# Attention scores: the rests of the keys kept twice, each copy on one half of the partitions with zeros on the other, so that both products of a head read 128 rows

## The chip, the cores and the metric

The kernel runs on one core of one Trainium2 chip. The metric is the device time of one execution in microseconds (us), the median over runs. Five engines work side by side: TensorE (PE; its weight loads are shown apart as PEld), VectorE (DVE), ScalarE (ACT), GpSimd (POOL) and SyncE (SP), which issues most of the DMAs.

## The reference, cut to what matters

Two transformer blocks are computed for 256 tokens of width 1024. The change lies in the attention of the first block. It has eight heads of 64 columns and two groups of keys and values, four heads to a group. For every query there are three sets of scores, each followed by a softmax and a weighted sum of values:

```python
logits_c = einsum('bgrsd,bgnd->bgrsn', qg, kc) * scale + bias    # 15 compressed keys
logits_s = einsum('bgrqd,bgqkd->bgrqk', q_b, ks) * scale + bias_s  # selected blocks
logits_w = einsum('bgrqd,bkgd->bgrqk', q_b, kw) * scale + bias     # window
o = g[..., 0:1] * o_c + g[..., 1:2] * o_s + g[..., 2:3] * o_w
```

Each score is a sum over the 64 columns of one head. All data are float32.

## The kernel before, in words

TensorE multiplies float32 numbers here in a shorter form (F32R). To keep the accuracy, every operand is split in a rounded part and a rest (`split`, lines 362 to 364: ACT copies the rounded part, DVE or POOL subtracts it from the source). A full product is then made of three: rounded by rounded, rounded by rest, rest by rounded (`mm3`).

**How the scores are laid out.** For head `h` the tile `q[:, h]` has the rounded queries on one half of its 128 partitions (the lower half for even heads, the upper one for odd heads) and the rests of the same queries on the other half (lines 858 to 860). The tile `k` of a branch (`ks` for the selected blocks, `kw` for the window) has two planes: plane 0 the rounded keys, the same on both halves, plane 1 the rests of the keys, the same on both halves (lines 866 to 872). The compressed keys `kc` are laid out in the same way (lines 765 and 766). So `dots` (lines 957 to 961) makes two products for each head: all 128 rows of `q` with plane 0, which gives the rounded queries and their rests times the rounded keys, and then 64 rows of `q`, the half with the rounded queries, with 64 rows of plane 1. The second takes 64 rows because the other half of `q[:, h]` holds rests, which must not be multiplied with the rests of the keys.

**Order around it.** `attend(tt)` is a generator for 128 queries. It is called for the second half of the tokens first (256 keys, `ns` is 2) and then for the first half (128 keys). Each makes one group of scores for `kc` (8 heads, 16 columns each) and then the groups of `ks` and `kw`: two groups of four heads each per branch for 256 keys, one group of eight heads per branch for 128 keys. A group begins with products of `flip` and `wp`, which put the bias into PSUM (line 1013), and goes on with `dots`. In a pair of heads (one even, one odd) the order is: 128 rows, 64 rows, 128 rows, 64 rows. The score groups write to PSUM tiles tagged `y` (4 buffers, 2 to a group), and `soft` (DVE maxima, ACT exponentials) of a group is issued behind the `dots` of the next group.

Between two groups `run(t)` puts filler work onto TensorE: the projections of the convolution branch (`conv_part`, products `pb<-hT,hl`) and later the output projection. How much is decided while the program is built, from planned prices (`AC`, `AS`, `AX_`, `AP`, `AP0`) and the planner's own count of the filler's time (`self.pe`); the products of `dots` are not in that count. In this stage only ACT's order is written by hand; the order of the other engines is the scheduler's. The filler's weights come over `Stream`: a DMA into 4 raw buffers, then a split into 3 buffers `hl`.

**Tiles touched.** `pct` (line 1041) is the tile that the compressed softmax is spread into, twice per call of the kernel, in a pool of its own (`sm`, 2 buffers). The pool `work` has a tag `xs` with 2 buffers of 128 x 1024, used by the norm at the start of the block and by the one at its end (`start`, `boundary`, `lead`).

Of the kernel before, what the change touches and what calls it, by code (L numbers as in the profile page):

```python
# [10 lines left out]
F32 = mybir.dt.float32  # L11
F32R = mybir.dt.float32r
# [3 lines left out]
AF = mybir.ActivationFunctionType  # L16
# [325 lines left out]
class Kern:  # L342
# [381 lines left out]
    def compress(self, p, pe, which):  # L724

        nc = self.nc
        z = self.tmp.tile([128, 2, 256], F32, tag="z", name=self.name("z"), bufs=2)
        for g in range(2):
            nc.scalar.activation(z[0:64, g], p[g * 64:(g + 1) * 64, :256], AF.Copy)
            nc.vector.tensor_copy(z[64:128, g, 0:255], p[g * 64:(g + 1) * 64, 1:256])  # L730
        blk = self.tmp.tile([128, 16, 2, 15], F32, tag="blk", name=self.name("blk"), bufs=2)
        for hf in range(2):
            src = z[:, :, 16 * hf:16 * hf + 240].rearrange("p g (n l two) -> p l g n two", l=8, two=2)[:, :, :, :, 0]
            b = self.vs(pe, 8 * hf, 8)
            for g in range(2):
                nc.vector.tensor_add(blk[:, 8 * hf:8 * hf + 8, g], src[:, :, g], b[:, :, None].to_broadcast([128, 8, 15]))  # L736
        br = self.tmp.tile([128, 2, 16, 30], F32R, tag="br", name=self.name("br"), bufs=2)
        bv = blk.rearrange("p l g n -> p l (g n)")
        self.split(br[:, 0], br[:, 1], bv)
        yield  # L740
        hid = self.tmp.tile([128, 2, 2, 16], F32, tag="hid", name=self.name("hid"), bufs=2)
        nc.gpsimd.memset(hid, 0.0)
        ph = self.pb()
        for i in range(4):
            w = self.st.get().rearrange("p h (l c) -> p h l c", l=4)
            for j in range(4):
                self.mm3(ph[:30, :256], (br[:, 0, 4 * i + j], br[:, 1, 4 * i + j]), (w[:, 0, j], w[:, 1, j]),
                         i + j == 0, i + j == 6)
            if i == 1:
                yield  # L750
        hr = self.tmp.tile([30, 256], F32, tag="hr", name=self.name("hr"), bufs=2)
        nc.scalar.activation(hr, ph[:30, :256], AF.Gelu_apprx_tanh)
        yield
        p = self.pb()
        for ht in range(2):
            self.tr(p[:, ht * 32:ht * 32 + 30], hr[:, ht * 128:(ht + 1) * 128])
        for ht in range(2):
            nc.vector.tensor_copy(hid[:, ht, :, :15], p[:, ht * 32:ht * 32 + 30].rearrange("p (g n) -> p g n", g=2))
        yield
        p2 = self.pb()  # L760
        if which == "k":
            for ht in range(2):
                self.mm(p2[:, :32], self.w2[:, ht, :128],
                        hid[:, ht].rearrange("p g n -> p (g n)"), ht == 0, ht == 1)
            self.kc = self.attn.tile([128, 2, 32], F32R, name="kc")
            self.split(self.kc[:, 0], self.kc[:, 1], p2[:, :32])
        else:
            hv = self.tmp.tile([128, 2, 2, 4, 16], F32, name="hv")
            for ht in range(2):
                nc.vector.tensor_copy(hv[:, ht], hid[:, ht][:, :, None, :].to_broadcast([128, 2, 4, 16]))  # L770
            for ht in range(2):
                self.mm(p2[:, :64], hv[:, ht].rearrange("p g r n -> p (g r n)"), self.w2[:, ht, 128:], ht == 0, ht == 1)
            self.vcb = self.attn.tile([128, 2, 64], F32, name="vcb")
            nc.vector.tensor_mul(self.vcb, p2[:, :64][:, None, :].to_broadcast([128, 2, 64]),
                                 self.c("hpar")[:, :, None].to_broadcast([128, 2, 64]))
# [42 lines left out]
    def block1(self, ctx):  # L818
        tc, nc, A = self.tc, self.nc, self.A
# [21 lines left out]
        with tc.manual_schedule(engines={mybir.EngineType.PE}):  # L841
# [11 lines left out]
            q = self.attn.tile([128, 8, 256], F32R, tag="q", name="q", bufs=1)  # L853
            for i in range(4):
                p = self.proj(self.st.get(), hT, S)
                for j in range(2):
                    r, o = slice(64 * j, 64 * j + 64), slice(64 - 64 * j, 128 - 64 * j)
# [5 lines left out]
        kd, vt = {}, {}  # L863
        for br in "sw":
            p = self.proj(self.st.get(), hT, S)
            k = self.attn.tile([128, 2, 2, 256], F32R, name=f"k{br}")
            for g in range(2):
                r = slice(g * 64, g * 64 + 64)
                o = slice(64 - g * 64, 128 - g * 64)
                self.split(k[r, 0, g], k[r, 1, g], p[r, :256])  # L870
                nc.scalar.activation(k[o, 0, g], k[r, 0, g].bitcast(F32), AF.Copy)
                nc.vector.tensor_copy(k[o, 1, g], k[r, 1, g].bitcast(F32))
            kd[br] = k.rearrange("p a g s -> p a (g s)")
            next(cv, None)
        pv = [self.pb(), self.pb()]
        for k0, k1 in VVG:
            w = self.st.get().rearrange("p h (k c) -> p h k c", c=280)
            for tt in range(2):
                t = slice(tt * 128, tt * 128 + 128)
# [15 lines left out]
        sm = ctx.enter_context(tc.tile_pool(name="sm", bufs=1))  # L895
# [52 lines left out]
        def half(h):  # L948
            return slice((h % 2) * 64, (h % 2) * 64 + 64)

        def attend(tt):
# [3 lines left out]
            t = slice(tt * 128, tt * 128 + 128)  # L955

            def dots(out, heads, k, c0, n, stop):
                for o, h in zip(out, heads):
                    r = half(h)
                    self.mm(o, q[:, h, t], k[:, 0, c0:c0 + n], False, False)  # L960
                    self.mm(o, q[r, h, t], k[r, 1, c0:c0 + n], False, stop)

            P = sm.tile([128, 2, 8, sw], F32, tag=f"P{tt}", name=self.name("P"), bufs=1)
            nm = self.small.tile([128, 16], F32, tag="nm", name=self.name("nm"), bufs=2)
# [3 lines left out]
            p = self.py()  # L968
            for j in range(2):
                o = p[:, 512 * j:512 * j + 64].rearrange("p (h n) -> p h n", h=4)  # L970
# [3 lines left out]
            for i in range(4):  # L974
                dots([p[:, 512 * j + 16 * i:512 * j + 16 * i + 16] for j in range(2)], (2 * i, 2 * i + 1), self.kc,
                     i // 2 * 16, 16, i == 3)
# [28 lines left out]
            for b, br in enumerate("sw"):  # L1005
                for gi in range(0, len(groups), 2):
                    y = self.py()
                    pv = [y[:, 512 * j:512 * j + 512].rearrange("p (h s) -> p h s", h=nh) for j in range(2)]
                    hss = groups[gi:gi + 2]
                    for j in range(2):  # L1010
                        hs = hss[j]
                        for hl in range(2):
                            self.mm(pv[j], self.flip, self.wp[:, hl, hs[0]:hs[-1] + 1:2, 256 - sw:256], hl == 0, False)
                    for i in range(nh):
                        hs = [hss[j][i] for j in range(2)]
                        dots([o[:, i] for o in pv], hs, kd[br], hs[0] // 4 * 256, sw, i == nh - 1)
                    late()
                    late = lambda b=b, hss=hss, pv=pv: soft(b, hss, pv)
                    yield AS
# [18 lines left out]
            p = self.pb()  # L1038
            self.tr(p[:, :128], pc.rearrange("p h n -> p (h n)"))
            late()  # L1040
            pct = sm.tile([128, 4, 128], F32, tag="pct", name=self.name("pct"), bufs=2)
            nc.vector.tensor_mul(pct, p[:, None, :128].to_broadcast([128, 4, 128]),
                                 self.c("hpair")[:, :, None].to_broadcast([128, 4, 128]))
            scale(*steps[0])
# [48 lines left out]
        with tc.manual_schedule(engines={E.Activation}):  # L1093
            a1, a0 = attend(1), attend(0)
            for t in till_none(a1):
                run(t)
            first = till_none(a0)
            for t in a1:
                run(t)
                t = next(first, None)  # L1100
                if t is not None:
                    run(t)
            for t in first:
                run(t)
            scored = True
            w3 = self.attn.tile([128, 3, 2, 1024], F32R, tag="wp", name="w3", bufs=1)
            w1 = self.attn.tile([128, 2, 1024], F32R, tag="q", name="w1", bufs=1)
            w2 = sm.tile([128, 2, 2, 1024], F32R, tag="P1", name="w2", bufs=1)
            self.st.spare = [w3[:, 0], w3[:, 1], w3[:, 2], w1, w2[:, 0], w2[:, 1]]
            for t in a0:  # L1110
                run(t)
            for _ in fl:
                pass
# [931 lines left out]
```

## Time and profile before

| what | value |
|---|---|
| median of 3 runs | 1535.54 us (1530.86 to 1537.42) |
| the profiled execution, its own time | 1540.11 us |
| its span in the profile | 1538.4 us |
| granted TensorE clock, mean over the span | 0.972 |
| PE busy | 1455.4 us (95%) |
| DVE, ACT, POOL busy | 1067.6, 807.3, 280.9 us |
| the stage of the scores | about 71 to 153 us |

The rows further down are from one profiled execution. In the timeline, each row is a run of like instructions: its start, the time from the first one's start to the last one's end, engine, line, operation, tiles written and read, the shape of the first of them, and their count. Matmuls overlap, so the time that one takes from TensorE is read as the start of the next row less the start of this one, by the count. Line 371 is the helper `mm`, through which nearly all products go.

### The profile page before, as it was taken

The page shows a single profiled execution, that of the slowest core. Times are in us where ns is not written, and L with a number is a line of the kernel's source. Part 1 is how long each engine was busy: PE and PEld are TensorE (multiplying, and loading weights), DVE is VectorE, ACT ScalarE, POOL GpSimd, SP SyncE. Part 2 cuts the span into 40 slices and gives each one's busy share as a digit, 9 for nine tenths or more (in the row PEclk, how much of TensorE's full clock was granted, in tenths as well). Part 3 has the DMA queues.
Part 4 walks back from the last instruction along what each step waited for, and adds up shares of the span by engine and source line. Part 5 has one row for each costly group of instructions (what it writes and reads, how often), then busy time and mean ns, then how long its engine had stood idle before and what let it go on. Part 6 is the DMA issues. An engine that isn't in the chain of part 4 may idle for free.

```text
span 1538.4 us, 29510 instructions
## 1 busy us (share of the span) xinstructions
PE 1455.4 (95%) x11884; PEld 1325.3 (86%) x11884; DVE 1067.6 (69%) x1979; ACT 807.3 (52%) x1282; POOL 280.9 (18%) x138
## 2 busy tenths in 40 slices
PE   5999899999888869998999999999999999999997
PEld 4979799998777768978999899999999998888886
DVE  6765777777579992974990699884555556777766
ACT  4734565555463344644445577774444445444554
POOL 3100320004353423025698200000000000000000
PEclk9998999999899989999999999999999999999999
DMA  6622445555332212354477444547555557877773
GB/s 206 238 91 76 149 164 181 192 183 201 117 114 67 79 56 76 131 193 141 159 227 231 156 166 159 169 158 219 192 183 188 191 191 270 244 243 242 241 243 127
DMA packets 93024, 263.50 MB, mean 171 GB/s; under 512 B 10271, under 2 KB 34975, under 8 KB 92760
## 3 DMA queue, kind: packets, MB, share of 16 engines
q1 hardware_dynamic: 77200, 243.80, 48.6%
q10 hardware_dynamic: 15688, 17.83, 3.4%
q8 instruction: 93, 1.52, 0.4%
q14 instruction: 43, 0.35, 0.1%
HBM read 247.67 MB, written 13.91 MB: 170 GB/s over the span
## 4 chain that ended last, share of the span: by engine, by line
PE 75%; DVE 16%; ACT 4%; DMA 2%; issue 2%; POOL 1%; SPq 0%; ACTq 0%; DVEq 0%; POOLq 0%
PE pb L371 39%; PE py L371 35%; DVE acc L1247 4%; DVE hl L364 2%; ACT hl L363 1%; PE pb L383 1%; DMA raw<-in_ws_dram 1%; POOL hl L364 1%; DVE m L1869 1%; DVE nc L425 0%; DMA x<-in_x_dram 0%; DVE blk L736 0%; ACT junk L515 0%; DVE nc L426 0%; DMA cst<-in_cst_dram 0%
## 5 line engine op out<-in xcount | busy, mean ns | idle before, releaser
L371 PE MATMUL pb<-hT,hl 128*128 128x256 f32 (+1 forms) x4944 | 630.8, 286 | 10.6 <-DVE qT L364 5.2
L371 PEld LDWEIGHTS pb<-hT,hl 128*128 128x128 f32 x4944 | 612.0, 192 | 19.2 <-issue 6.3
L363 ACT ACTIVATE hl<-raw 128x1024 fp32r<-128x1024 f32 x412 | 434.2, 1054 | 232.5 <-issue 162.8
L364 DVE TENSOR_TENSOR hl<-raw,hl 128x1024 fp32r<-128x1024 f32 (+1 forms) x317 | 389.3, 1228 | 111.1 <-ACT hl L363 110.9
L371 PE MATMUL py<-hl,coef 128*128 128x512 f32 x1536 | 356.4, 390 | 0.2 <-DVE coef L364 0.2
L371 PEld LDWEIGHTS py<-hl,coef 128*128 128x128 f32 x1536 | 285.5, 188 | 59.7 <-DVE coef L364 0.6
L364 POOL TENSOR_TENSOR hl<-raw,hl 128x1024 fp32r<-128x1024 f32 x95 | 236.8, 2499 | 354.7 <-ACT hl L363 234.1
L1922 ACT ACTIVATE act<-pb 128x256 f32<-128x256 f32 x128 | 49.3, 385 | 166.1 <-PE pb L371 166.1
L2001 POOL TENSOR_TENSOR end<-end,end 128x512 f32<-128x512 f32 x2 | 2.6, 1279 | 665.0 <-DVE end L1999 663.5
L371 PE MATMUL py<-hT,hl 128*128 128x272 f32 (+1 forms) x768 | 118.2, 304 | 1.6 <-POOL hl L364 1.6
L371 PEld LDWEIGHTS py<-hT,hl 128*128 128x128 f32 x768 | 103.5, 198 | 8.3 <-issue 4.8
L364 DVE TENSOR_TENSOR coef<-act,coef 128x256 fp32r<-128x256 f32 x128 | 54.0, 423 | 72.5 <-ACT coef L363 72.5
L1926 DVE TENSOR_TENSOR act<-act,G 128x256 f32<-128x256 f32 x128 | 53.8, 420 | 34.4 <-ACT act L1922 33.2
L1247 DVE SCALAR_TENSOR_TENSOR acc<-UU,vt,acc 128x256 f32<-128x256 f32 x120 | 75.5, 670 | 0.7
L1882 ACT ACTIVATE G<-py 128x512 f32<-128x512 f32 x64 | 67.4, 1143 | 3.0 <-PE py L371 3.0
L1869 DVE TENSOR_TENSOR m<-e,gg 128x1536 bf16<-128x1536 bf16 x64 | 60.6, 953 | 0.7
L371 PE MATMUL py<-m,e 128*128 128x128 bf16 x768 | 52.8, 219 | 1.0 <-DVE m L1869 0.9
L363 ACT ACTIVATE coef<-act 128x256 fp32r<-128x256 f32 x128 | 51.7, 404 | 3.3 <-DVE act L1926 3.3
L1865 DVE TENSOR_TENSOR e<-gi,iota 128x1024 bf16<-128x1024 bf16 x64 | 43.6, 688 | 12.6 <-PE py L371 12.5
L371 PEld LDWEIGHTS <-e 128*128 128x128 bf16 x768 | 44.3, 97 | 4.4 <-DVE m L1869 2.4
L371 PE MATMUL py<-hl,gu 128*128 128x512 f32 x192 | 47.3, 393 | 0.4 <-DVE hl L364 0.2
L371 PEld LDWEIGHTS py<-hl,gu 128*128 128x128 f32 x192 | 34.9, 188 | 7.7 <-DVE hl L364 0.5
(416 smaller groups left out, 1380.7 us busy)
## 6 DMA issues: line engine op xcount, KB each, us to landing
raw<-in_ws_dram SPq DMA_DIRECT2D x172, 512.0 KB, 3.4
raw<-in_ut_dram SPq DMA_DIRECT2D x128, 512.0 KB, 3.4
raw<-in_ev_dram SPq DMA_DIRECT2D x128, 512.0 KB, 4.2
ad<-act ACTq DMA_DIRECT2D x90, 128.0 KB, 3.1
act<-ad SPq DMA_DIRECT2D x90, 128.0 KB, 3.1
wf<-fd ACTq DMA_DIRECT2D x2, 800.0 KB, 4.9
x<-in_x_dram SPq DMA_DIRECT2D x2, 512.0 KB, 6.1
xd<-x ACTq DMA_DIRECT2D x1, 1024.0 KB, 4.2
```

The lines of the kernel that those rows point to most:

```text
L363: self.nc.scalar.activation(h, src, AF.Copy)
L364: (eng or self.nc.vector).tensor_sub(l, src, h.bitcast(F32))
L371: self.nc.tensor.matmul(out, lhsT, rhs, start=start, stop=stop, skip_group_check=True)
L383: self.nc.tensor.transpose(out, in_, self.ident[p0:p0 + n, p0:p0 + n])
L1247: nc.vector.scalar_tensor_tensor(acc[:, i], UU[:, i, 16 + j:272 + j], self.v("cw", 4 * j + i), acc[:, i], op0=OP.mult, op1=OP.add)
L1865: nc.vector.tensor_tensor(e.rearrange("p c a i j -> p (c a) i j"), gi[:, b].rearrange("p c (a j) -> p (c a) j", j=2)[:, :, None, :].to_bro ...
L1869: nc.vector.tensor_mul(m, e[:, 0][:, None].to_broadcast([128, 3, 2, 128, 2]), gg[:, b].rearrange("p k (a j) -> p k a j", j=2)[:, :, :, Non ...
L1882: nc.scalar.activation(G[:, :, 4 * b:4 * b + 4].rearrange("p a t -> p t a"), p.rearrange("p (t a) -> p t a", t=4), AF.Copy)
L1922: nc.scalar.activation(a, p[:, :S], AF.Gelu)
L1926: nc.vector.tensor_mul(a, a, self.G[:, c])
L2001: nc.gpsimd.tensor_mul(t[:, tt], x[:, tt, cols[1]], g[:, cols[1]])
```

## The change

`k` gets three planes: plane 0 as before, plane 1 with the rests on the lower half and zeros on the upper one, plane 2 with zeros on the lower half and the rests on the upper one. POOL writes the zeros; ACT and DVE write the same number of copies as before. `kc` gets three planes in the same way; its rest is now made by two DVE subtractions of 64 partitions each in place of one of 128. The second product of `dots` takes all 128 rows of `q` with plane 1 for even heads and plane 2 for odd heads, so the half of `q` with rests meets zeros. `pct` moves from its own tag to the tag `xs` of the pool `work`.

```diff
-            self.kc = self.attn.tile([128, 2, 32], F32R, name="kc")
-            self.split(self.kc[:, 0], self.kc[:, 1], p2[:, :32])
+            self.kc = self.attn.tile([128, 3, 32], F32R, name="kc")
+            nc.gpsimd.memset(self.kc[:, 1:].bitcast(F32), 0.0)
+            nc.scalar.activation(self.kc[:, 0], p2[:, :32], AF.Copy)
+            for j in range(2):
+                r = slice(64 * j, 64 * j + 64)
+                nc.vector.tensor_sub(self.kc[r, 1 + j], p2[r, :32], self.kc[r, 0].bitcast(F32))
...
-            k = self.attn.tile([128, 2, 2, 256], F32R, name=f"k{br}")
+            k = self.attn.tile([128, 3, 2, 256], F32R, name=f"k{br}")
             for g in range(2):
                 r = slice(g * 64, g * 64 + 64)
                 o = slice(64 - g * 64, 128 - g * 64)
-                self.split(k[r, 0, g], k[r, 1, g], p[r, :256])
+                nc.gpsimd.memset(k[o, 1 + g].bitcast(F32), 0.0)
+                self.split(k[r, 0, g], k[r, 1 + g, g], p[r, :256])
                 nc.scalar.activation(k[o, 0, g], k[r, 0, g].bitcast(F32), AF.Copy)
-                nc.vector.tensor_copy(k[o, 1, g], k[r, 1, g].bitcast(F32))
+                nc.vector.tensor_copy(k[o, 2 - g, g], k[r, 1 + g, g].bitcast(F32))
...
                 for o, h in zip(out, heads):
-                    r = half(h)
                     self.mm(o, q[:, h, t], k[:, 0, c0:c0 + n], False, False)
-                    self.mm(o, q[r, h, t], k[r, 1, c0:c0 + n], False, stop)
+                    self.mm(o, q[:, h, t], k[:, 1 + h % 2, c0:c0 + n], False, stop)
...
-            pct = sm.tile([128, 4, 128], F32, tag="pct", name=self.name("pct"), bufs=2)
+            pct = self.work.tile([128, 8, 128], F32, tag="xs", name=self.name("pct"), bufs=2)[:, :4]
```

## Rows read from the trace of the kernel before

**Rows 1.** The page: the chain that ended last, shares of the span by engine.

```profile
PE 75%; DVE 16%; ACT 4%; DMA 2%; issue 2%; POOL 1%; SPq 0%; ACTq 0%; DVEq 0%; POOLq 0%
```

**Rows 2.** Busy time by stretch; columns: stretch, length, each engine's busy time, clock, DMA.

```profile
50.00:71.30 21.30, 20.49 (x165) 18.99 (x164) 18.45 (x29) 14.54 (x24) 4.21 (x2) 1.00 0.65 217
71.30:99.40 28.10, 28.10 (x161) 22.67 (x160) 14.74 (x34) 14.25 (x38) 0.00 (x0) 1.00 0.34 124
99.40:131.50 32.10, 32.10 (x162) 27.76 (x161) 17.75 (x50) 10.58 (x35) 0.00 (x0) 0.79 0.20 66
...
153.00:170.00 17.00, 14.82 (x75) 11.28 (x74) 14.34 (x23) 13.20 (x29) 2.55 (x2) 1.00 0.61 201
```

**Rows 3.** Instructions on tile q: durations (min/median/max), first and last start, shapes.

```profile
L371 PEld LDWEIGHTS py<-kc,q x32: 182/184/192, 71.6 to 102.8; 128*128 128x128 f32 x16, 64*128 64x128 f32 x16
L371 PE MATMUL py<-kc,q x32: 256/273/277, 71.6 to 102.8; 128*128 128x16 f32 x16, 64*128 64x16 f32 x16
...
L371 PE MATMUL py<-ks,q x32: 220/328/385, 78.1 to 114.3; 128*128 128x256 f32 x8, 64*128 64x256 f32 x8, 128*128 128x128 f32 x8, 64*128 64x128 f32 x8
```

**Rows 4.** Timeline of TensorE, 71 to 100 us, attend of the second half.

```profile
71.65 3.33 PE L371 MATMUL py<-kc,q 128*128 128x16 f32 x16
74.91 2.40 PE L371 MATMUL pb<-hT,hl 128*128 128x256 f32 x18
...
78.07 2.46 PE L371 MATMUL py<-ks,q 128*128 128x256 f32 x8
80.47 2.37 PE L371 MATMUL pb<-hT,hl 128*128 128x256 f32 x18
...
87.53 1.09 PE L371 MATMUL py<-wp,flip 128*128 128x512 f32 x4
```

**Rows 5.** Timeline of TensorE, 96 to 135 us, attend of the first half.

```profile
110.56 4.09 PE L371 MATMUL py<-ks,q 128*128 128x128 f32 x16
114.57 2.93 PE L371 MATMUL pb<-hT,hl 128*128 128x256 f32 x12
...
121.77 4.64 PE L371 MATMUL py<-kw,q 128*128 128x128 f32 x16
126.33 4.21 PE L371 MATMUL pb<-hT,hl 128*128 128x256 f32 x18
130.34 1.05 PE L383 MATMUL pb<-ident,P 128*128 128x128 f32 x4
```

**Rows 6.** Timeline of TensorE, 716 to 753 us: products of 128 rows alone.

```profile
718.05 2.79 PE L371 MATMUL pb<-kT,qT 128*128 128x128 f32 x24
720.68 5.89 PE L371 MATMUL pb<-hT,hl 128*128 128x256 f32 x48
726.40 2.79 PE L371 MATMUL pb<-kT,qT 128*128 128x128 f32 x24
```

**Rows 7.** Busy time in short stretches; columns as in rows 2.

```profile
104.18:107.59 3.41, 3.41 (x13) 2.57 (x13) 3.21 (x10) 1.46 (x2) 0.00 (x0) 0.50 0.00 0
114.42:117.83 3.41, 3.41 (x16) 3.30 (x17) 1.01 (x3) 0.00 (x0) 0.00 (x0) 0.50 0.39 143
124.66:131.49 6.83, 6.83 (x29) 6.30 (x29) 3.23 (x12) 0.72 (x4) 0.00 (x0) 0.50 0.17 67
131.49:134.90 3.41, 3.41 (x31) 3.41 (x31) 1.92 (x2) 1.53 (x3) 0.00 (x0) 1.00 0.03 5
```

**Rows 8.** Timeline of POOL, 0 to 110 us; idle time before in brackets.

```profile
0.90 2.66 POOL L884 MEMSET v<- 128x3072 f32 x1
10.90 2.35 POOL L364 TENSOR_TENSOR hl<-raw,hl 128x1024 fp32r<-128x1024 f32 x1 [7.34 <-ACT hl L363]
...
57.77 2.40 POOL L364 TENSOR_TENSOR hl<-raw,hl 128x1024 fp32r<-128x1024 f32 x1 [5.95 <-ACT hl L363]
```

**Rows 9.** Timeline of DVE, 50 to 68 us: the preparation of the keys.

```profile
57.82 2.50 DVE L872 CAST ks<-ks 64x256 fp32r<-64x256 f32 x1
```

**Rows 10.** Timeline of ACT, 77 to 94 us: last exponential of the first ks group.

```profile
84.41 0.22 ACT L997 ACTIVATION_READ_ACCUMULATOR P<-py,nm 128x1 f32 x1
```

## The prediction

> **What bounds the kernel now.** I read the page first: the chain of work that ended last lies on TensorE for three quarters of the span [rows 1]. So a saving counts where TensorE is the one that is waited for. The table by stretch says where that is around the change: from 71.3 to 131.5 us TensorE is busy for the whole of both stretches, while DVE is busy for 14.74 of 28.10 and 17.75 of 32.10 us, ACT for less, and the DMA engines for a third or a fifth [rows 2]. No other engine and no transfer holds this stage; it lasts as long as its products take. Before it, from 50 to 71.3 us, TensorE has 0.8 us idle and DVE is nearly full (18.45 of 21.30); behind it, from 153 to 170 us, TensorE is idle for 2.2 us [rows 2]. Faster scores don't shorten these two.
>
> Then the timeline, by starts. The 16 products of `kc` start at 71.65 and the next work at 74.91: 204 ns each, for 16 columns. Eight products of `ks` with 256 columns take 78.07 to 80.47, 300 ns each [rows 4]. Sixteen with 128 columns take 110.56 to 114.57, 251 ns each [rows 5]. Half of them read 128 rows and half 64, one after the other [rows 3]. Elsewhere in the same trace, products of 128 rows that follow each other take 110 ns at 128 columns (718.05 to 720.68 for 24) and 119 ns at 256 columns (720.68 to 726.40 for 48) [rows 6]. So the columns are not what costs 200 to 300 ns here. What differs is that the row count changes at every product. I read both changes as slow: had only the 64-row products been slow, a pair of 600 ns would split into 119 and 481, four times the usual price for one product.
>
> [...]
>
> **The change, part by part.**
>
> *The products.* There are 96: 32 of 16 columns (two groups of 16), 32 of 256 columns (four groups of 8), 32 of 128 columns (two groups of 16); `kw` is like `ks` [rows 3]. Now: 2 x 3.26 + 4 x 2.40 + 4.01 + 4.56 = 24.7 us [rows 4, 5]. After, all with 128 rows: at 128 columns 32 x 0.110 = 3.5, at 256 columns 32 x 0.119 = 3.8 [rows 6]. For 16 columns I take the price of 128 columns as the upper bound, 3.5 again; the lower bound is nothing, and I stay at the upper one, since the 204 ns of today are hardly less than the 251 of 128 columns, so the columns are the small part. Sum 10.8, a saving of 13.9 us. TensorE alone sets the stage, so all of it should arrive.
>
> [...] The rows show a product with 128 rows every 119 ns, though a weight load of this kernel lasts 182 to 192 ns, so a load must run beside the product before it [rows 3, 6]. [...]
>
> *The clock.* At half clock 18 products of 256 columns take 126.33 to 130.34, 223 ns each against 119 [rows 5, 6]: 47% of such a stretch is lost. The three stretches are 13.65 us [rows 7], so 6.4 us; 0.6 of it lies in the second group of 16 (4.56 against 4.01) and is counted already, which leaves 5.8 as the upper bound; the lower one is nothing. I take 5.3, since not all work there are such products. Why nearly all: every fall stands behind 3.3 to 4.6 us of alternation; the runs of 2.4 us had none behind them (1.00 from 71.3 to 99.4), and of the two `kc` groups of 3.3 us one had none [rows 2, 4]. Afterwards no group takes more than 1.8 us.
>
> *The zeros.* Four memsets on POOL of 64 x 512 and one of 128 x 64. The memset of `v` took 2.66 us for 3072 columns, so 0.45 each and 2 us together as an estimate. They wait for nothing; `v`'s memset, which stands later in the program than they do, ran at 0.90 us, and POOL was then idle for 7.34 us until 10.90 [rows 8]. That hides them. Without this cover they would fall among the key copies: a DVE copy that took 2.50 us at 57.82 sat beside a POOL split of 2.40 us from 57.77 [rows 8, 9]. Four copies held up by 0.45 each would be 1.8 us where DVE is nearly full. Bounds 0 and 1.8; I take 0.1, by the place of `v`'s memset. No DMA is added, and no queue of SP is passed.
>
> *DVE.* One more subtraction for `kc`, of 32 columns. A mean DVE instruction of that stretch takes 18.45 / 29 = 0.64 us [rows 2]: bounds 0 and 0.6, and I take 0.2 for so narrow a one. The copies of `k` stay the same in number and size.
>
> *`pct` in the tag `xs`.* The program writes it between the two norms that use this tag, with all the scores between the first norm and `pct`, and the weighted sums of values between `pct` and the second. These hide the exchange: cost 0. Without this cover it would be the wait for one product that reads `pct`, under 1 us.
>
> *New waits.* With 32.1 us shrinking to about 20 in the second stretch, DVE's 17.75 us fill nearly nine tenths of it [rows 2]. Next to be late are the PSUM buffers of the scores: the third group of this branch pair starts at 87.53, and the buffers that it takes are free when the exponentials of the first `ks` group end at 84.63, 2.9 us earlier [rows 4, 10]. These exponentials stand behind filler that comes earlier too; between them and 87.53 lies one group that gets shorter by 1.45, so 1.4 us of slack remain. Behind a late group the filler would queue, and with it all of TensorE. Bounds 0 and half of the saving; I take 1.0 us.
>
> Sum: 13.9 + 5.3 - 0.1 - 0.2 - 1.0 = 17.9 us less. The profiled execution has a span of 1538.4 and took 1540.11 us; from there the result would be 1522.2. It was 4.6 us slower than the median shown, 1535.54, and a forecast for a median starts at that: 1517.6 us. Behind this stage TensorE bounds most of the rest [rows 1], and the weight stream runs ahead by a fixed number of buffers, so the gain should be kept to the end.
>
> **The rivals.**
>
> *The clock stays low.* The products get faster, but the falls stay or come at other places, since products of 16 columns still stream little. For it: the first fall stands behind a `kc` group. Against it: the other `kc` group had none behind it [rows 2, 4]. Saving 13.9 - 1.3, 1523 us.
>
> *A wait takes the place.* TensorE stands before the next score group, or before a filler product whose split DVE has not yet done. For it: DVE at nine tenths. Against it: 1.4 us of slack at the tightest place I found. If half of the 17.9 goes: 1526.6 us.
>
> *Nothing, or little, changes.* The price hangs on something that the change keeps, say the two PSUM banks that a pair of heads takes in turn. For it: no row shows these very operands with 128 rows only. Against it: 110 and 119 ns for other operands [rows 6]. 1535.5 us. [...] The trace has 300 against 119 ns where the row counts alternate. [...]
>
> *Slower.* The scheduler orders DVE, POOL and TensorE, and new work can turn its order over. It hurts where a DVE copy or scaling of this stage falls beside a POOL split: 2.50 us in place of a mean of 0.64, so 1.9 each [rows 2, 9]. Ten of them eat the gain; fourteen would give 1517.6 + 26.6 = 1544 us. Against it: POOL has no work at all from 71.3 to 131.5 us [rows 2].
>
> **How the numbers follow.** The likeliest, 1517.6 us, has 0.60 and its own range 1512 to 1523: below, 5.8 for 5.3, no new waits, and one or two falls of the clock fewer further on (3.41 us at 47%, 1.6 each); above, one or two more, and 3 us of new waits. Clock stays low 0.20. A wait takes half 0.07. Nothing or little 0.09. Slower 0.04. The range 1510 to 1528 holds the first three but for their far ends. About 0.5%, 7.7 us, is what a measurement of this kernel can tell from no change: faster 0.87, the same 0.09, slower 0.04.
>
> **What would show it.** In the profile after: all 96 products with 128 rows; 16 of 16 columns in 1.8 us, 8 of 256 columns in 1.0, 16 of 128 columns in 1.8; a granted clock of 1.00 through the stage; the memsets on POOL before 10 us; the 60.2 us of the two score stretches down to about 42, and the end of the span earlier by as much. I am wrong if the products still take 200 ns or more, if TensorE is idle ahead of score groups or transposes there, or if the stage shrinks and the span does not.

## The result, and the profile after

The kernel with the change takes 1518.42 us, the median of 6 runs (1515.12 to 1521.99); the kernel before, in runs beside them, 1536.28 (6 runs, 1528.5 to 1537.53). The ratio is 0.9888 with an interval of 0.9871 to 0.9905: 17.9 us less by the medians. The forecast was 17.9 us less, at 1517.6. The profiled execution took 1517.68 us with a span of 1515.9.

The page of the kernel after: the span, the busy time by engine and the chain that ended last.

```profile
span 1515.9 us, 29516 instructions
...
PE 1433.8 (95%) x11884; PEld 1312.1 (87%) x11884; DVE 1067.5 (70%) x1980; ACT 806.8 (53%) x1282; POOL 282.5 (19%) x143
...
PE 75%; DVE 17%; ACT 4%; issue 2%; DMA 1%; POOL 1%; ACTq 0%; DVEq 0%; POOLq 0%
```

The chain is what it was [rows 1]: TensorE still sets three quarters of the end. The gain lies in the stage of the scores. From the first product of `kc` to the last transpose of `pc` it took 80.99 us before (71.65 to 152.63) and takes 61.12 now (73.41 to 134.53), 19.9 less. The busy time in this stage, in two stretches; columns as in [rows 2]:

```profile
73.41:99.40 25.99, 25.99 (x204) 24.75 (x203) 19.21 (x48) 17.32 (x48) 0.00 (x0) 1.00 0.44 151
99.40:134.53 35.13, 35.13 (x296) 34.75 (x295) 25.68 (x55) 17.19 (x39) 0.00 (x0) 1.00 0.32 106
```

TensorE is busy for every microsecond of both, as before, so it still sets the stage alone: no wait has come in. The clock is granted at 1.00 throughout, where it was 0.79 in the second stretch [rows 2]. DVE fills 73% of the second (25.68 of 35.13).

The timeline of TensorE, to be laid beside [rows 4, 5]:

```profile
73.41 1.93 PE L371 MATMUL py<-kc,q 128*128 128x16 f32 x16
75.19 2.37 PE L371 MATMUL pb<-hT,hl 128*128 128x256 f32 x18
...
78.34 1.12 PE L371 MATMUL py<-ks,q 128*128 128x256 f32 x8
79.29 2.29 PE L371 MATMUL pb<-hT,hl 128*128 128x256 f32 x18
...
101.53 1.90 PE L371 MATMUL py<-ks,q 128*128 128x128 f32 x16
103.27 1.63 PE L371 MATMUL pb<-hT,hl 128*128 128x256 f32 x12
...
108.93 1.90 PE L371 MATMUL py<-kw,q 128*128 128x128 f32 x16
110.67 2.35 PE L371 MATMUL pb<-hT,hl 128*128 128x256 f32 x18
```

By starts: 16 products of 16 columns in 1.78 us (111 ns each, 204 before), eight of 256 columns in 0.95 (119, was 300), sixteen of 128 columns in 1.74 (109, was 251). The instructions on `q` (columns as in [rows 3]) show why: all have 128 rows now. One product by itself lasts somewhat less than it did (256 against 273 ns at the median for `kc`, 282 against 357 on average for those of `ks` with 128 rows and 256 columns, with ends that the profile models); the distance of the starts shrank by far more.

```profile
L371 PE MATMUL py<-kc,q x32: 256/256/257, 73.4 to 95.6; 128*128 128x16 f32 x32
...
L371 PE MATMUL py<-ks,q x32: 221/278/285, 78.3 to 103.2; 128*128 128x256 f32 x16, 128*128 128x128 f32 x16
```

One thing went against the change, and ahead of the stage: the first product of `ohd` starts at 18.94 us in place of 16.84, and the first of `kc` at 73.41 in place of 71.65. The timeline of POOL after, where [rows 8] showed one memset and then a single split:

```profile
1.03 1.09 POOL L875 MEMSET ks<- 64x512 f32 x2
...
2.26 1.09 POOL L875 MEMSET kw<- 64x512 f32 x2
3.30 2.65 POOL L890 MEMSET v<- 128x3072 f32 x1
10.80 2.35 POOL L364 TENSOR_TENSOR hl<-raw,hl 128x1024 fp32r<-128x1024 f32 x1 [4.85 <-ACT hl L363]
13.39 2.34 POOL L364 TENSOR_TENSOR hl<-raw,hl 128x1024 fp32r<-128x1024 f32 x1 [0.24 <-ACT hl L363]
15.68 0.29 POOL L840 CAST flip<-cst 128x128 fp32r<-128x128 f32 x1
```

And that of DVE, where the first norm is worked out in instructions on single numbers:

```profile
10.79 2.38 DVE L425 SCALAR_TENSOR_TENSOR nc<-nc,nc 128x1 f32<-128x1 f32 x1
13.21 0.16 DVE L426 SCALAR_TENSOR_TENSOR nc<-nc 128x1 f32<-128x1 f32 x1
13.40 2.35 DVE L427 SCALAR_TENSOR_TENSOR nc<-nc,nc 128x1 f32<-128x1 f32 x1
```

The memsets lie in POOL's idle time and delay no split. But the two splits now follow each other, and each starts with one of DVE's small instructions, which takes 2.4 us where the one between them takes 0.16. Before, the second split came later, at 15.80, behind the work on `omu`, `oka` and `flip`, and only one small instruction was caught. TensorE waits for what DVE makes of these numbers (`xg`), 5.30 us now and 3.01 before. DVE and TensorE before, then TensorE now:

```profile
10.98 2.28 DVE L425 SCALAR_TENSOR_TENSOR nc<-nc,nc 128x1 f32<-128x1 f32 x1
...
13.49 0.16 DVE L427 SCALAR_TENSOR_TENSOR nc<-nc,nc 128x1 f32<-128x1 f32 x1
...
14.94 1.97 PE L383 MATMUL pb<-ident,xg 128*128 128x128 f32 x8 [3.01 <-DVE xg L793]
```

```profile
17.04 1.97 PE L383 MATMUL pb<-ident,xg 128*128 128x128 f32 x8 [5.30 <-DVE xg L797]
```

So the difference of the two profiled spans, 1538.4 - 1515.9 = 22.5 us, is 19.9 of the stage, less 1.8 ahead of it, and some 4 behind it. The 1.8 are not the price of the zeros alone: between `ohd` and `kc` the clock was at 0.50 for 6.83 us before (from 35.91) and for 3.41 after (from 39.64). Of the 4, two lie at the end of the attention: before, a scaling of `P` took 2.42 us at 167.46, beside a POOL split, and TensorE then idled for 2.00. The other two lie near 700 us, where one fall of the clock was 6.83 us long before and 3.41 after. In another execution of the kernel after (after_again) such a slow scaling was there (2.44 us at 148.87), so I don't count the 4 as the change's. They are nearly the 4.6 us by which the profiled execution of before was slower than its median.

### The profile page after: what moved, and what is told of

The parts are those of the page before. It is cut to its first block, busy times and chain, and to the rows that moved or that the text cites. A ratio compares the mean times of both kernels' runs of the same rounds, so it can differ in the third digit from the quotient of the medians.

```text
span 1515.9 us, 29516 instructions
## 1 busy us (share of the span) xinstructions
PE 1433.8 (95%) x11884; PEld 1312.1 (87%) x11884; DVE 1067.5 (70%) x1980; ACT 806.8 (53%) x1282; POOL 282.5 (19%) x143
## 4 chain that ended last, share of the span: by engine, by line
PE 75%; DVE 17%; ACT 4%; issue 2%; DMA 1%; POOL 1%; ACTq 0%; DVEq 0%; POOLq 0%
PE pb L371 39%; PE py L371 35%; DVE acc L1252 4%; DVE hl L364 2%; ACT hl L363 1%; PE pb L383 1%; DMA raw<-in_ws_dram 1%; POOL hl L364 1%; DVE m L1874 1%; DVE nc L425 0%; DVE blk L736 0%; DMA x<-in_x_dram 0%; ACT junk L515 0%; DVE nc L427 0%; DVE nc L426 0%
```

## The experiments

They ask three things: whether the row counts of the products are the cause, what the clock falls for, and what the zeros cost. The stage is measured as above in each; "half clock" are the lengths granted at 0.50 in it; "products" is the sum over the 96 by starts.

| kernel | median us (runs) | ratio to before, interval | first `ohd` | stage us | products us | half clock us |
|---|---|---|---|---|---|---|
| before | 1536.28 (6) | | 16.84 | 80.99 | 24.67 | 13.65 |
| after | 1518.42 (6) | 0.9888, 0.9871 to 0.9905 | 18.94 | 61.12 | 10.85 | 0 |
| layout_only | 1540.99 (12) | 1.003, 1.0012 to 1.0048 | 18.40 | 80.82 | 24.78 | 13.65 |
| group_order | 1518.44 (6) | 0.9876, 0.9843 to 0.991 | 16.64 | 61.02 | 10.04 | 0 |
| short_runs | 1535.0 (12) | 0.9995, 0.9974 to 1.0016 | 16.64 | 80.97 | 24.34 | 13.65 |
| zeros_dve | 1514.36 (6) | 0.9863, 0.9836 to 0.9891 | 16.60 | 61.13 | 10.85 | 0 |
| kc_only | 1531.75 (10) | 0.9989, 0.9964 to 1.0013 | 18.36 | 76.47 | 21.49 | 10.24 |
| k_only | 1522.4 (8) | 0.9928, 0.9896 to 0.9961 | 18.55 | 65.75 | 13.79 | 3.41 |
| spread_runs | 1540.62 (10) | 1.004, 1.0012 to 1.0068 | 16.35 | 75.88 | 23.11 | 3.41 |
| after_again | 1514.23 (6) | 0.9891, 0.9848 to 0.9933 | 18.62 | 61.13 | 10.85 | 0 |
| after_third | 1518.51 (4) | 0.989, 0.9867 to 0.9913 | 18.64 | 61.12 | 10.85 | 0 |
| zeros_dve_2 | 1517.0 (5) | 0.9852, 0.9826 to 0.9879 | 16.29 | 61.12 | 10.85 | 0 |
| group_order_2 | 1516.16 (6) | 0.9865, 0.9839 to 0.9891 | 16.44 | 61.02 | 10.04 | 0 |

Each ratio is to the runs of the kernel before on the same chip: layout_only to zeros_dve beside 23 runs at 1536.1, the next four beside 27 at 1534.65, the last three beside 11 at 1536.87.

**layout_only**: all of the change's copies, zeros and tags, but the second product of a head goes back to its 64 rows.

```diff
-                    self.mm(o, q[:, h, t], k[:, 1 + h % 2, c0:c0 + n], False, stop)
+                    r = half(h)
+                    self.mm(o, q[r, h, t], k[r, 1 + h % 2, c0:c0 + n], False, stop)
```

> The changed kernel with its three planes, its memsets, its second subtraction for kc and pct in the tag xs, but with the second product of each head again on 64 rows. If the row counts of the products are the cause (my theory), nothing is gained: the 96 products take 24.7 us as before, the granted clock falls in the stage as before, and the time is that of the kernel before plus the 2.1 us that the changed kernel lost at its start, 1536 to 1540 us. If the planes, the place of pct or the order of the other engines made the gain (rival), the time stays near 1518 us.

Nothing of the gain is left. The stage takes 80.82 us, and the whole is 0.3% slower than before. Timeline of TensorE of this kernel:

```profile
70.31 3.33 PE L371 MATMUL py<-kc,q 128*128 128x16 f32 x16
...
78.26 2.46 PE L371 MATMUL py<-ks,q 128*128 128x256 f32 x8
80.64 2.38 PE L371 MATMUL pb<-hT,hl 128*128 128x256 f32 x18
```

These are the numbers of before, 3.26 and 2.40 us by starts [rows 4]. So the row counts carry the gain; the new tiles by themselves bring none, and the first product of `ohd` comes 1.6 us later than before. The first of `kc` comes earlier all the same (70.31), since in this profiled execution, the fastest of its 12 runs (1531.99 us), no fall of the clock stands ahead of the stage. Of the three falls in the stage one stands behind the first `kc` group here (74.40), where before it was the second (104.18 [rows 7]; the last product of `kc` starts at 102.8 [rows 3]): which of the two groups draws one differs.

**kc_only and k_only**: the 128 rows only for the products of `kc` (16 columns), and only for those of `ks` and `kw`. The edit of kc_only stands below; k_only has `n > 16` in it.

```diff
-                    self.mm(o, q[:, h, t], k[:, 1 + h % 2, c0:c0 + n], False, stop)
+                    r = slice(0, 128) if n == 16 else half(h)
+                    self.mm(o, q[r, h, t], k[r, 1 + h % 2, c0:c0 + n], False, stop)
```

> The changed kernel, in which only the compressed keys take 128 rows in both products; the second products of ks and kw are on 64 rows again. My theory that the price is of each change of the row count: the 32 kc products take 3.6 us in place of 6.5 and the other 64 stay at 18.2, so 21.8 us in all; the fall of the clock behind the second kc group goes and those behind the two long groups of 128 columns stay. With 2 us lost at the start the time is about 1534 us. Rival: if the falls depend on the products of 16 columns alone, they all go, and the time is about 1530 us.

> The other part: ks and kw take 128 rows in both products, the second products of kc are on 64 rows. My theory: the 64 products of ks and kw take 7.3 us in place of 18.2, kc stays at 6.5, so 13.8 us in all; the falls behind the two long groups go, the one behind the second kc group may stay. Time about 1523 us with 2 us lost at the start. With kc_only the savings on the products have to add up to that of the whole change, 13.9 us; if they don't (rival), something common to both parts carries the price.

The stages fall by 4.5 and 15.2 us, 19.7 together where the whole change brought 19.9: the parts add up, and neither hides the other. The totals, 0.9989 and 0.9928 times before, are these less the 2 us at the start, within their intervals. Of the falls of the clock, kc_only lost the one behind the second `kc` group and kept the others; k_only kept only that one (99.18, 3.41 us). The stretch from 98 to 131 us, kc_only and then k_only, columns as in [rows 2]:

```profile
98.00:131.00 33.00, 33.00 (x196) 29.54 (x196) 20.75 (x54) 13.34 (x39) 0.00 (x0) 0.84 0.20 65
```

```profile
98.00:131.00 33.00, 33.00 (x254) 32.02 (x254) 22.93 (x57) 15.01 (x36) 0.00 (x0) 0.95 0.28 96
```

TensorE is full in both, and the clock falls behind the groups that still alternate: a mean of 0.84 with those of `ks` and `kw`, 0.95 with those of `kc`.

**group_order**: the kernel before with its 64-row products and without zeros; only the order inside a group of scores is changed. First come all of its 128-row products, then all of its 64-row ones, whose halves of the partitions take turns. The calls hand over the lists of a whole group.

```diff
-            def dots(out, heads, k, c0, n, stop):
-                for o, h in zip(out, heads):
-                    r = half(h)
-                    self.mm(o, q[:, h, t], k[:, 0, c0:c0 + n], False, False)
-                    self.mm(o, q[r, h, t], k[r, 1, c0:c0 + n], False, stop)
+            def dots(todo):
+                for out, heads, k, c0, n, stop in todo:
+                    for o, h in zip(out, heads):
+                        self.mm(o, q[:, h, t], k[:, 0, c0:c0 + n], False, False)
+                for out, heads, k, c0, n, stop in todo:
+                    for o, h in zip(out, heads):
+                        r = half(h)
+                        self.mm(o, q[r, h, t], k[r, 1, c0:c0 + n], False, stop)
```

> The kernel before, without zeros: in each group of scores all products with 128 rows stand first and all with 64 rows behind them, the halves in turn, so that the row count changes twice in a group in place of 16 or 8 times. If what costs is the change of the row count (my theory), the 96 products take about 11 to 13 us, the clock stays up, and the time is within 3 us of the changed kernel, 1516 to 1521 us. If each product of 64 rows is slow by itself, whatever stands before it (rival; in block two eight products of 64 rows and 272 columns in a row start 254 ns apart in the trace of before), the 48 of them take 200 to 250 ns each, the sum is about 16 us, and the time is 1523 to 1530 us.

The stage takes 61.02 us and the whole 0.9876 of before: as much as the change brings, with half of the products still on 64 rows. Timeline of TensorE:

```profile
71.35 1.58 PE L371 MATMUL py<-kc,q 128*128 128x16 f32 x16
72.86 2.39 PE L371 MATMUL pb<-hT,hl 128*128 128x256 f32 x18
...
76.02 1.06 PE L371 MATMUL py<-ks,q 128*128 128x256 f32 x8
77.01 2.40 PE L371 MATMUL pb<-hT,hl 128*128 128x256 f32 x18
```

The starts of the eight `ks` products in the trace, in ns (the last three are the next work, of 128 rows), and below them those of before:

```
group_order  76018 76137 76250 76366 | 76575 76578 76796 76800 | 77007 77229 77352
before       78074 78283 78593 78908 79217 79531 79842 80157 | 80468 80691 80809
```

Four products of 128 rows come 113 to 119 ns apart. The change to 64 rows takes 209, the change back 207, some 90 ns more than that. The distance behind each change is long as well: 218 from the first pair of 64 rows to the second, and 222 from the first product of the next work to its second, where 123 follows. So a change costs some 190 ns, spread over two distances. Between the changes, the two halves of a pair start 3 and 4 ns apart, that is, together. Before, every product was a change, and from the second distance on they are 309 to 315 ns: 190 more than usual, since each pays the second part of one change and the first of the next. The groups of 16 give the same sums: at 128 columns 206 and 160 in place of 111 and 110, 145 more, against 142 in the alternation; at 16 columns 185 and 129 in place of 112 and 109, 93 more, against 93.

The weight loads show where this time goes. Where the row count stays, as for `ks` in the kernel after and the filler behind it, the load of a product starts 110 to 120 ns ahead of it behind a product of 256 columns, beside that product. At a change it starts 1 or 2 ns ahead of its own product: in the alternation at every product but the first, in group_order only at the first pair of 64 rows and at the next work.

So the price hangs on the change of row count and not on the 64 rows, as they stand here in pairs on both halves. Products of 64 rows on one half only, in a row, were not run in this stage; those of block two that the expectation names have operands of plain float32, not F32R, and start 333 to 334 ns apart behind the change and 229 to 230 afterwards in the traces of before and after.

**short_runs**: the kernel before, with the groups of 16 of the first half cut into two runs of 8, and half of the filler moved between them. My theory was then that the length of an unbroken alternation makes the clock fall.

```diff
                      i // 2 * 16, 16, i == 3)
+                if tt == 0 and i == 1:
+                    run(AC // 2)
...
-            yield AC
+            yield AC if tt else AC // 2
...
+                        if tt == 0 and i == 1:
+                            run(AS // 2)
...
-                    yield AS
+                    yield AS if tt else AS // 2
```

> The kernel before with its alternation of 128 and 64 rows, but in the attend of the first half each group of 16 products is cut in two runs of 8 with 6 filler products between them; the filler behind it is shorter by as many. If the falls of the clock come from long runs of alternation (my theory), they are gone, and the time is 5 to 6 us less than before, 1529 to 1532 us, with the 96 products at 24 us as before. If the falls hang on the kinds of products as such or on where they fall in time (rival), the clock still falls in the stage and the time is that of before within 2 us.

The theory fell: again 13.65 us at half clock, and a ratio of 0.9995. The two runs of a `ks` group started 1.93 and 2.53 us ahead of the work behind them (the second already in part at half clock), about the 2.4 us behind which the clock had stayed up before.

**spread_runs**: cut further, into four runs of 4, with filler between all of them (`i < 3` in place of `i == 1` above).

> The kernel before, with the long groups cut further than in short_runs: runs of 4 alternating products (about 1 us) with 6 or 12 filler products (0.7 or 1.4 us) between them; later filler comes earlier for it. In short_runs the clock still fell, so the length of one run is not the cause. If the share of alternating products in a stretch is (my theory now), this share drops from two thirds to about one half, near that of the attend of the second half (2.4 of 5.5 us), which had no fall: no half clock between 95 and 135 us, and the sum of the 96 products is 24 us without a single one at 400 ns. If the falls hang on something else in that stretch (rival), such as the products of 16 and 128 columns with few columns in flight, the clock still falls for about 10 us there.

In the changed half the clock now stays at 1.00, though half of the products in each group still have 64 rows. The stretch of short_runs, then of spread_runs, and of the latter the end of the attention:

```profile
98.00:131.00 33.00, 33.00 (x170) 28.87 (x169) 18.40 (x52) 11.44 (x37) 0.00 (x0) 0.79 0.19 64
```

```profile
98.00:131.00 33.00, 33.00 (x221) 29.31 (x220) 20.64 (x49) 14.73 (x40) 0.00 (x0) 1.00 0.28 96
...
145.96:175.00 29.04, 25.02 (x115) 19.69 (x114) 20.03 (x36) 15.83 (x35) 8.57 (x4) 0.90 0.50 164
```

The one fall left in its stage, at 73.55 us, stands behind the first `kc` group, which this edit doesn't touch. So the falls of this stage came with the alternation (half clock for 13.65 us with all of it, 10.24 in kc_only, 3.41 in k_only, none in after and group_order), and one long run of it is not needed. From short_runs to spread_runs the runs got shorter and there is more filler between them; these runs don't tell the two apart. The total got no better, 1.004 times before: the filler was used up early, and at the end of the attention TensorE is idle for 4.0 us of 29.04, 3.25 of them in one wait for DVE's part of `pt`. DVE was held up there, from 168.04 to 170.30, by an instruction on one number per partition beside a POOL split, as at the start of the kernel after. The last transpose of `P` comes 28 us behind the last of `pc`, where it is 15 to 18 in the other kernels. The stage gained 5.1 us, and this end lost more.

**zeros_dve**: the kernel after, with the memsets of the zeros on DVE.

```diff
-            nc.gpsimd.memset(self.kc[:, 1:].bitcast(F32), 0.0)
+            nc.vector.memset(self.kc[:, 1:].bitcast(F32), 0.0)
...
-                nc.gpsimd.memset(k[o, 1 + g].bitcast(F32), 0.0)
+                nc.vector.memset(k[o, 1 + g].bitcast(F32), 0.0)
```

> The changed kernel with its five memsets of zeros on DVE in place of POOL. In the changed kernel POOL runs its second weight split before three small operations that stood ahead of it before, and a DVE instruction of the start norm stands beside it for 2.35 us in place of 0.16. If that order is what cost 2.1 us at the start (my theory), it goes back with the memsets off POOL, the first kc product starts near 71.5 us in place of 73.4, and the time is 2 us less than the changed kernel, 1515 to 1517 us. If the delay came from elsewhere, such as the transfers at the start (rival), the first kc product stays at 73 to 74 us and the time near 1518.

POOL's order is that of before again, timeline of POOL:

```profile
11.04 2.35 POOL L364 TENSOR_TENSOR hl<-raw,hl 128x1024 fp32r<-128x1024 f32 x1 [7.49 <-ACT hl L363]
14.48 0.24 POOL L1163 TENSOR_SCALAR omu<-vt 128x14 f32<-128x14 f32 x1 [1.09 <-DMA vt<-in_vec_dram]
...
15.56 2.35 POOL L364 TENSOR_TENSOR hl<-raw,hl 128x1024 fp32r<-128x1024 f32 x1
```

On DVE, the memsets and the small instructions that answer to those of the kernel after:

```profile
1.11 1.11 DVE L875 MEMSET ks<- 64x512 f32 x2
...
10.72 0.22 DVE L425 SCALAR_TENSOR_TENSOR nc<-nc,nc 128x1 f32<-128x1 f32 x1
10.97 0.16 DVE L426 SCALAR_TENSOR_TENSOR nc<-nc 128x1 f32<-128x1 f32 x1
11.17 2.24 DVE L427 SCALAR_TENSOR_TENSOR nc<-nc,nc 128x1 f32<-128x1 f32 x1
```

Only one of them is slow, and the first product of `ohd` starts at 16.60. In every kernel run here that has the zeros on POOL it starts at 18.4 to 18.9, in every other at 16.3 to 16.8. The 2 us reach the stage: with the clock at 0.50 for as long ahead of it (6.83 us), the first product of `kc` starts at 73.13 and 73.59 with the zeros on POOL (after_again, k_only), and at 70.71 to 71.65 without (before, zeros_dve_2, group_order, group_order_2). The ratio is 0.9863; whether the 2 us arrive at the end is what the repeats were for.

**after_again, after_third, zeros_dve_2 and group_order_2** are the kernel after (twice), zeros_dve and group_order once more, the last three on one chip.

> The changed kernel itself once more, as a measure for the others in this call and for how far one profiled execution differs from the next. If the 2 us at the start come from the order of POOL (my theory), the DVE instruction beside the second weight split of POOL is again at 2.3 us and the first ohd product again 2 us later than in the kernel before. The stage from the first kc product to the last transpose of pc again takes 61.1 us, without half clock. If the stage's time without a fall was chance (rival), it takes 62.7 us or more. Ratio to before 0.987 to 0.991.

> The changed kernel beside zeros_dve and group_order on one chip, since the intervals of the earlier calls overlap. If the order of POOL at the start is a loss of the program (my theory), the first ohd product comes again 1.8 to 2.1 us later than with the zeros on DVE, and the median is 2 us above that of zeros_dve. If it is chance of the transfers (rival), the three start alike and the medians agree within 1 us.

> As before: the ohd product at 16.6 us, the stage 61.1 us, ratio to the kernel before about 0.986 to 0.988, 2 us below the changed kernel of the same call.

> As before: the 96 products in 10.0 us, the stage 61.0 us, the ohd product at 16.6 us since POOL's order is that of the kernel before; ratio 0.986 to 0.989, level with zeros_dve within 2 us.

The kernel after is at 0.9888, 0.9891 and 0.989 of before; zeros_dve at 0.9863 and 0.9852; group_order at 0.9876 and 0.9865. The lead of zeros_dve, 0.25 to 0.4% or some 4 to 6 us, is on the side that the 2 us at the start would have it, but the intervals overlap, and the medians on the one chip differ by 1.5 us. Zeros_dve and group_order can't be told apart. All three versions are clearly faster than before; zeros_dve has the lowest ratios, and group_order needs neither the zeros nor the third copy.

## Why the prediction was right

**The products.** Forecast 24.7 to 10.8 us, measured 24.67 to 10.85, and all 13.8 arrived, since TensorE was busy throughout the stage. That the columns are a small part, and that 16 columns cost as much as 128, held: 111 against 109 ns. The reading behind it, that both changes of row count are slow, is borne out by group_order, where pairs of 64-row products cost no more than others once the change lies behind them, and by layout_only, where the changes alone bring the old price back.

**The clock.** Forecast 5.3 us, at most 5.8. All three falls, 13.65 us at 0.50 before [rows 7], went: the clock is at 1.00 through the stage. What the stage gained beside the products is 19.86 - 13.82 = 6.0, but not all of it is the clock: the second part of the change behind each group fell on the filler, 222 ns to its second product in place of 118 to 123 behind a group of 256 columns. An estimate from the starts behind all eight groups, before and after, is 0.55 us; the forecast had no term for it. That leaves about 5.5 for the clock, within the bounds. What stands as the reason in the forecast, that falls come behind 3.3 us or more of unbroken alternation, was wrong: short_runs had none so long in that half and kept 13.65 us. The sign came out because the change ends all alternation, whatever its length.

**The zeros: the step whose size failed.** "I take 0.1, by the place of `v`'s memset" was right on the place (0.8 to 3.4 us, with POOL idle for 4.85 us until 10.80) and wrong on the cost. What was measured is 2.1 us at the first `ohd` product, of which 1.8 were left at the first of `kc`. The memsets held up no split by the time that they take; with them in the program, the scheduler put POOL's other instructions in another order. This is the mechanism of the slower rival, a DVE instruction beside a POOL split, once, and at a place that I hadn't looked at. With the zeros on DVE it was gone.

**New waits.** Forecast 1.0 us, measured none. The stretch that answers to the 32.1 us of before did shrink to 20.5 (93.50 to 114.02), and DVE fills 16.32 of them, four fifths of it where the forecast kept all 17.75 us and came to nearly nine tenths. TensorE is never idle in it.

**DVE's extra subtraction and `pct`.** 0.2 and 0 in the forecast. TensorE has no idle time in the stage, so neither shows there; by itself neither was measured.

**The sum.** 13.8 + 6.0 - 1.8 = 18.0 us against 17.9 measured and 17.9 forecast. The zeros cost 1.7 more than forecast; against that, the waits had 1.0 and the subtraction 0.2 for nothing, the clock gave 0.2 more, and 0.55 came from the filler behind the groups. These errors cancelled, and the total was better than its terms. It was luck too that the medians agree so closely, since the interval of the ratio allows 14.6 to 19.8 us.

**The rivals.** "The clock stays low" did not come: 1.00 through the stage, with all 32 products of 16 columns in it. "A wait takes the place" did not come either in this kernel; spread_runs shows what it looks like. "Nothing, or little, changes" is refuted for these very operands: products of 128 rows start every 109 to 119 ns in the trace after, where the alternating ones stood 204 to 300 ns apart before, and since their weight loads take 187 to 192 ns there, a load runs beside the product before it. "Slower" came once, at 2 us instead of fourteen times.

## What to carry to other kernels

Price a product by its neighbours as well as by its shape: read the distance of starts, and look for a row count that changes from one product to the next (300 against 119 ns here, at 256 columns), and for weight loads that start only with their own product. Sorting the products of a group by row count gave here what padding with zeros gave, without the zeros. Put new work on an idle engine only after looking at what its other instructions stand beside, since a scheduler can turn their order; and when a clock falls on an engine that never waits, as to 0.50 here, look at what the engine is made to do there.

## What the runs showed of the hardware that was not expected

- Two 64-row products on opposite halves of the partitions start 2 to 5 ns apart in group_order. The next pair follows 106 to 110 ns later at 128 and 16 columns; the first step behind the change is 160 and 129 there, and 218 to 220 at 256.
- A change of row count costs some 190 ns at 256 columns, 142 to 145 at 128 and 93 at 16, alone or in a row of changes. It falls on two distances, since the weight load at a change starts 1 or 2 ns ahead of its own product instead of 110 to 120 (at 256 columns).
- The granted clock fell to 0.50 in stretches in which TensorE was never idle in the profile: 33.00 busy of 33.00 us at a mean of 0.79. These falls needed no wait that the profile shows.
- A DVE instruction on one number per partition took 1.95 to 2.4 us instead of 0.16 to 0.22 when it started beside a split of 128 x 1024 on POOL with most of it to go (2.28 in before, 2.38 and 2.35 in after, 1.95 and 2.33 in after_again, 2.24 in zeros_dve), and ended with that split. This holds for SCALAR_TENSOR_TENSOR: over all traces, 46 that started with more than 0.25 us of a split to go ended 12 to 20 ns behind it. The 88 TENSOR_SCALAR instructions on one number beside such splits took 0.14 to 0.22 us.
